# Tiles rounded to 256-byte lines, and 528 columns cut into 256 and 272

## The chip, the cores and the metric

One core of a Trainium2 chip runs the whole program. The metric is the device time of one execution in microseconds, from the chip. Three runs of the kernel before gave 2609.26, 2610.55 and 2611.42 us; the median is 2610.55 us.

## The reference

The reference is three blocks of a small language model, in float32, for one sequence of 512 tokens with a width of 1024. Sixteen learned tokens are put ahead of it for the first block, which therefore works on 528 tokens.

```
first_block:  h = h + 0.5*rmsnorm(swiglu(rmsnorm(h)))      # 528 tokens, hidden width 2816
              m = hybrid_mixer(rmsnorm(h))                 # stick-breaking and latent attention, gated
              h = h + rmsnorm(m)
              h = h + 0.5*rmsnorm(swiglu(rmsnorm(h)))      # only the 512 tokens are needed
second_block, layer 0: gated linear recurrence and matrix memory (rglru, mlstm)
              layer 1: sliding-window attention with sinks
              both:    x = x + conv_ffn(rms_norm(x))       # hidden width 3072
                       x = x + sigmoid(rms_norm(x) @ w_gate) * (p @ w_proj)
```

Nearly all of the arithmetic is products of activations with weight matrices of 1024, 2816 or 3072 rows or columns.

## The kernel before, in words

Activations lie transposed: features on the 128 partitions, in chunks of 128, and tokens along the free axis. A weight block of 128 outputs is the stationary operand, 128 by 128 for each chunk of features; the tokens are the moving operand, 512 columns at a time, or 528 columns in two equal pieces of 264 (`banks2`, L247 to L251), since a PSUM bank holds 512 columns.

Float32 accuracy comes from a split. Every operand is kept as a high and a low part of type float32r, and a product is three: high by high, high by low, low by high. So `mm` (L273) issues, per chunk of 128 features, three weight loads with three products of 512 columns; with two pieces it issues six of 264, and each of the six has its own weight load. `lin_first` (L296) is the same for the first blocks of a stage, `mm_tok` (L283) has the tokens on the stationary side. In the rows, `xh` and `xl` are the two parts of a stage's input, `whi` and `wlo` those of the weights, and a name such as `l<-xh,whi` is a product of the two into PSUM tile `l`.

Weights stream: `wdma` (L254) fetches up to 512 KB from DRAM into one of two raw buffers, ScalarE makes `whi` (L265) and VectorE makes `wlo` (L266), each with three buffers. PSUM has six banks for the large products (`l`). VectorE and ScalarE take the results out, apply the norm's factor, convolution and activation, and split the result into the two parts of the next input. GpSimd does a few multiplications and the sums of squares. All transfers are issued from the SP queue. Engines other than TensorE are ordered by a scheduler which follows program order with a priority for the weight split.

The stages, with the names of the moving operands in the rows: feed-forward 1 (`xh`, `xl`, then `hh`, `hl`; 264 columns), the mixer (`cqh`, `ysbh`, `ymh`, `ooh`), feed-forward 2 (`xh`, `hh`; 512 columns), the recurrence layer, then twice a convolution feed-forward (`xh`, then `chh`, `chl`) and a gated embedding (`xh`), and between the two of them the window attention (`yh`, `yl`).

SBUF tiles come from pools stacked from the left and from the right end of each partition, in the order in which the code opens them; each tile starts where the one before it ends, rounded up to 32 bytes. So the start of an operand depends on all small tiles ahead of it. Read from the built program, these are the starts of the float32r operands, as the rest after division by 256, and how many 512-column products have each difference (moving less stationary, rest by 256):

| operand | start before | moving less stationary | products of 512 columns |
|---|---|---|---|
| weights `whi`, `wlo` | 160 | | |
| `chh`, `chl` | 160 | 0 | 1152 |
| `ooh`, `yh`, `ymh` and their low parts, one embedding input | 224 | 64 | 504 |
| all others: `xh` and `xl` (128 or 192), `hh` of feed-forward 2 (192), `cqh`, `ysbh` and so on | several | 32, 96, 160 or 224 | 6222 |

The 3552 products of 264 columns have all eight differences, about 450 each, because a chunk of 528 columns is 2112 bytes long. The steps between chunks of 512 columns (2048 bytes) and between chunks of a weight block (512 bytes) change none of the rests.

Of the kernel before, what the change touches and what calls it, by code (L numbers as in the profile page):

```python
# [21 lines left out]
HT = TM // 2  # L22
EPS = 1e-6
# [3 lines left out]
WB = (2, 3)  # buffers of raw and of split weights  # L27
# [12 lines left out]


def _wt(w):
    """[K, N] -> [N/128, 128, K]: per block of 128 outputs, K in chunks of 128 rows on the partitions."""
    k, n = w.shape
    return np.ascontiguousarray(w.reshape(k // P, P, n // P, P).transpose(2, 1, 0, 3).reshape(n // P, P, k))


def _wr(w, per):
    """[K, N] -> [K/128/per, 128, per*N]: rows in chunks of 128 on the partitions, per chunks side by side."""
    k, n = w.shape  # L50
    return np.ascontiguousarray(w.reshape(k // P // per, per, P, n).transpose(0, 2, 1, 3).reshape(k // P // per, P, per * n))
# [6 lines left out]
def _swap(w, half):  # L58
    """Swaps the two halves of every group of 2*half columns."""
# [12 lines left out]
def prep(inp):  # L72
# [85 lines left out]
    sink = a["at_sinks_2"][0].reshape(4, 2, 2).transpose(0, 2, 1).reshape(1, 16)  # per group: heads 0, 2, 1, 3  # L158
# [5 lines left out]
def consts():  # L164
    i = np.arange(P)
    c = {}
    # stick breaking: key strictly before the query; rows are queries
    c["m_sb"] = np.where(i[None, :] < i[:, None], 0.0, NEG)
    # latent attention: a query sees its whole chunk of 64
    c["m_mla"] = np.where(i[None, :] // 64 <= i[:, None] // 64, 0.0, NEG)  # L170
    # sliding window: previous block, own block
# [21 lines left out]


class Kern:
# [4 lines left out]
    # scalar engine, with the table sets in program order  # L200
# [31 lines left out]
    # PSUM: per phase, banks for the large products (l), short-lived ones (a), scores (z)  # L232
# [14 lines left out]
    def banks2(self):  # L247
        """two banks for TM columns: matmul pieces and evacuation pieces (psum, view of a [P, TM] tile)"""
        b = [self.bank(), self.bank()]
        segs = [(b[s][:, :HT], s * HT, (s + 1) * HT) for s in range(2)]  # L250
        return segs, [(b[s][:, :HT], (lambda t, s=s: t[:, s * HT:(s + 1) * HT])) for s in range(2)]  # L251

    # weights: raw load, then an exact split in two float32r parts
# [19 lines left out]
    def mm(self, segs, w, x, kc, k0=0, m=P, first=True, last=True):  # L273
        """segs: (psum, c0, c1); w: (hi, lo) with kc chunks of m columns; x: (hi, lo) tiles [P, k, t]"""
# [8 lines left out]
    def mm_tok(self, pss, x, ws, per, n):  # L283
        """tokens on the partitions: x as the stationary side; pss: (psum, c0, c1) per block of tokens"""
# [11 lines left out]
    def lin_first(self, srcs, x, kc, c0=0, wide=False, two=False):  # L296
        """several blocks of outputs at a time, for chunks of x that are still being made: all of them (wide), or the last"""
# [19 lines left out]
    def lin2(self, src, x, kc, m=P):  # L317
        """one block of outputs over all TM tokens, in two banks: (psum, c0, c1)"""
# [6 lines left out]
    def rsqrt_small(self, pool, out, x, scale, name):  # L325
        """out = 1/sqrt(x*scale + eps) for a few columns, in the tables of exp and log, with a Newton step"""
# [12 lines left out]
    def rstd(self, acc, tt, tb, dim, pool_r, name="r"):  # L339
        """acc [P, tt]: per token sums over the partitions -> 1/sqrt(mean + eps): tokens on partitions, and broadcast in PSUM"""  # L340
# [12 lines left out]
        # pieces (psum, c0, c1)  # L353
# [10 lines left out]
    def pool(self, st, name, bufs=1, side=None, **kw):  # L364
        return st.enter_context(self.tc.tile_pool(name=name, bufs=bufs, reuse_waits="tile", side=side or self.side, **kw))

    def norm(self, hs, gname, tt, side, upd=None, tb=P):
        """Opens the next phase on a side of SBUF: x = h*g split in two parts, without the 1/rms, which fin() gives:
        n.rs broadcast [P, tt], n.rt with tokens on the partitions. upd: per chunk a call that brings h up to date"""
# [29 lines left out]
    def post(self, fs, g, hs, tt, last=None):  # L399
        """h += rmsnorm(fs)*g, as one call per chunk; the squares of the chunks are gathered here"""  # L400
# [18 lines left out]
    def begin(self, st):  # L419
        nc, d = self.nc, self.d  # L420
        self.side = "left"
        cp = self.pool(st, "cst")
# [921 lines left out]
```

## Time and profile before

| | |
|---|---|
| median of three runs | 2610.55 us |
| span of the profiled execution, first to last instruction | 2605.1 us |
| what lies around the span, against that median | 5.45 us |
| PE busy | 2554.4 us, 98% |
| weight loads (PEld) busy | 2083.0 us, 80% |
| DVE, ACT, POOL busy | 1356.4, 978.9, 311.2 us |
| mean DMA rate | 92 GB/s |

PE is the TensorE matmul queue, PEld its weight loads, DVE VectorE, ACT ScalarE, POOL GpSimd. Products are pipelined: one is listed with its whole duration although the next starts long before it ends. What a product costs in a gapless stretch is therefore the step from its start to the next start, and that is read by dividing the time between a first and a last start by the number of steps between them. A float32 product (not float32r) has two records.

### The profile page before, as it was taken

Reading aid. Unit: us, or ns where it says so; the run is one execution under the profiler, and the core shown is the slowest. Engines: PE = TensorE matmul, PEld = TensorE weight load, DVE = VectorE, ACT = ScalarE, POOL = GpSimd, SP = SyncE. Lnnn points to the kernel's source line nnn. Section 1 sums busy time; section 2 is a strip of 40 time slices with the busy share of each in tenths; the row PEclk is TensorE's granted clock in tenths of the full one; section 3 lists DMA queues with packets and bytes.
Section 4 is the critical chain, followed back from the end, with each engine's and each line's share of the span. In section 5 each row is a group of like instructions: output and inputs, shape, how many; then the busy total and the mean of one; then the engine's idle time right before and its main releaser. Section 6 shows DMA issues by size and latency. Waiting matters only on the chain.

```text
span 2605.1 us, 33169 instructions
## 1 busy us (share of the span) xinstructions
PE 2554.4 (98%) x13330; PEld 2083.0 (80%) x13334; DVE 1356.4 (52%) x2108; ACT 978.9 (38%) x1561; POOL 311.2 (12%) x250
## 2 busy tenths in 40 slices
PE   8999999999999999999999999999999899999999
PEld 8999997776667788888777788888888578888887
DVE  5333347455575642334678655355475755535544
ACT  4222234343653632223534633223343553322332
POOL 3101101011002110101100111001122111100110
PEclk9999999999999999999999999999999999999999
DMA  3222233211103323233322322332333113233232
GB/s 136 90 93 87 98 97 125 73 57 57 52 30 114 125 97 97 87 99 98 110 81 90 121 89 93 93 101 92 91 108 99 57 49 123 92 94 104 88 92 97
DMA packets 76340, 239.43 MB, mean 92 GB/s; under 512 B 9045, under 2 KB 11349, under 8 KB 75929
## 3 DMA queue, kind: packets, MB, share of 16 engines
q1 hardware_dynamic: 76184, 237.30, 28.1%
q8 instruction: 105, 1.72, 0.3%
q14 instruction: 51, 0.41, 0.1%
HBM read 225.72 MB, written 8.40 MB: 90 GB/s over the span
## 4 chain that ended last, share of the span: by engine, by line
PE 88%; DVE 5%; issue 3%; ACT 3%; POOL 1%; DMA 1%; SPq 0%; DVEq 0%; POOLq 0%; ACTq 0%
PE l L280 75%; PE l L307 3%; PE a L623 2%; PE z L647 1%; PE l L293 1%; PE a L612 1%; DVE h L226 1%; DVE xl L383 1%; PE a L361 1%; DVE wlo L266 1%; POOL gm L226 0%; ACT whi L265 0%; PE s L1250 0%; PE a L346 0%; POOL acc L226 0%
## 5 line engine op out<-in xcount | busy, mean ns | idle before, releaser
L265 ACT CAST whi<-wraw 128x1024 fp32r<-128x1024 f32 (+4 forms) x440 | 430.0, 978 | 1150.8 <-PE l L280 942.1
L280 PE MATMUL l<-xh,whi 128*128 128x512 f32 (+3 forms) x2368 | 793.7, 361 | 0.5 <-DVE sbk L226 0.5
L280 PE MATMUL l<-xl,whi 128*128 128x512 f32 (+3 forms) x2368 | 789.6, 359 | 0.0
L280 PE MATMUL l<-xh,wlo 128*128 128x512 f32 (+3 forms) x2368 | 788.4, 359 | 0.0
L266 DVE TENSOR_TENSOR wlo<-wraw,whi 128x1024 fp32r<-128x1024 f32 (+4 forms) x440 | 503.7, 1146 | 286.7 <-ACT whi L265 278.2
L280 PEld LDWEIGHTS l<-xh,whi 128*128 128x128 f32 (+1 forms) x2368 | 419.0, 188 | 75.2 <-issue 4.9
L280 PEld LDWEIGHTS l<-xh,wlo 128*128 128x128 f32 (+1 forms) x2368 | 419.6, 188 | 72.2 <-issue 1.9
L280 PEld LDWEIGHTS l<-xl,whi 128*128 128x128 f32 (+1 forms) x2368 | 419.9, 187 | 70.9 <-issue 2.0
L226 POOL TENSOR_TENSOR acc<-acc,sq 128x512 f32<-128x512 f32 (+1 forms) x63 | 98.6, 1565 | 472.4 <-ACT sq L205 435.1
L280 PE MATMUL l<-chh,whi 128*128 128x512 f32 x384 | 149.4, 389 | 0.0
L280 PE MATMUL l<-chl,whi 128*128 128x512 f32 x384 | 149.4, 389 | 0.0
L280 PE MATMUL l<-chh,wlo 128*128 128x512 f32 x384 | 149.4, 389 | 0.0
L226 POOL TENSOR_TENSOR t<-g,xrs 128x528 f32<-128x528 f32 (+1 forms) x44 | 75.6, 1718 | 571.3 <-ACT g L215 571.3
L280 PE MATMUL l<-hh,whi 128*128 128x264 f32 (+1 forms) x528 | 141.3, 322 | 0.0
L280 PE MATMUL l<-hl,whi 128*128 128x264 f32 (+1 forms) x528 | 141.1, 322 | 0.0
L280 PE MATMUL l<-hh,wlo 128*128 128x264 f32 (+1 forms) x528 | 140.7, 321 | 0.0
L226 POOL TENSOR_TENSOR cc<-cc,xrs 128x512 f32<-128x512 f32 x48 | 63.2, 1317 | 601.1 <-ACT cc L215 601.1
L226 DVE TENSOR_TENSOR t<-l,t 128x264 f32<-128x264 f32 (+1 forms) x66 | 32.3, 516 | 151.6 <-PE l L280 148.2
L226 DVE TENSOR_TENSOR cz<-l,xrs 128x512 f32<-128x512 f32 x48 | 33.2, 691 | 123.4 <-PE l L280 119.2
L226 DVE TENSOR_TENSOR g<-l,xrs 128x264 f32<-128x264 f32 (+1 forms) x66 | 32.3, 515 | 124.4 <-PE l L280 119.9
L280 PEld LDWEIGHTS l<-hl,whi 128*128 128x128 f32 x528 | 87.7, 188 | 8.1
L280 PEld LDWEIGHTS l<-hh,wlo 128*128 128x128 f32 x528 | 87.7, 188 | 8.0
(342 smaller groups left out, 3252.6 us busy)
## 6 DMA issues: line engine op xcount, KB each, us to landing
wraw<-in_up SPq DMA_DIRECT2D x96, 512.0 KB, 3.4
wraw<-in_dn SPq DMA_DIRECT2D x64, 384.0 KB, 3.1
wraw<-in_ffn_g SPq DMA_DIRECT2D x44, 512.0 KB, 3.5
wraw<-in_ffn_u SPq DMA_DIRECT2D x44, 512.0 KB, 3.4
wraw<-in_ffn_d SPq DMA_DIRECT2D x32, 448.0 KB, 3.3
wraw<-in_hy SPq DMA_DIRECT2D x20, 512.0 KB, 3.5
wraw<-in_ffn_d SPq DMA_DIRECT2D x16, 512.0 KB, 3.5
wraw<-in_gate SPq DMA_DIRECT2D x16, 512.0 KB, 3.4
```

The costliest lines, as they stand in the source:

```text
L226: return (eng or self.nc.vector).tensor_tensor(out, a, b, op=op)
L265: nc.scalar.copy(hi, raw)
L266: nc.vector.tensor_tensor(lo, raw, hi, op=ALU.subtract)
L280: self.nc.tensor.matmul(ps, a[:, k * m:(k + 1) * m], b[:, k0 + k, c0:c1], start=first and k == 0 and pi == 0, stop=last and k == kc - 1 an ...
L293: self.nc.tensor.matmul(ps[:c1 - c0, :n], a[:, k, c0:c1], b[:, j * n:(j + 1) * n], start=k == 0 and pi == 0, stop=k == nk - 1 and pi == 2)
L307: self.nc.tensor.matmul(ps, a[:, k * P:(k + 1) * P], b[:, k, t0:t1], start=k == 0 and pi == 0, stop=k == kc - 1 and pi == 2)
L361: nc.tensor.matmul(p[:, c - a:c - a + w], r[:w, i:i + 1].to_broadcast([w, P]), self.ident[:w, :w], start=True, stop=True)
L383: nc.vector.scalar_tensor_tensor(n.x[1][:, k, :], hs[k], g, n.x[0][:, k, :], op0=ALU.mult, op1=ALU.subtract)
L612: nc.tensor.transpose(pt[:kk, j * P:(j + 1) * P], probs[hh][:, i * P:i * P + kk], self.ident)
L623: nc.tensor.matmul(po[64 * hh:64 * hh + 64, :], vt[:kk, i, (2 * c + hh) * 64:(2 * c + hh + 1) * 64], where[(i, hh)], start=i == 0, stop=i ...
L647: nc.tensor.matmul(ps, q, k[:, a:b], start=True, stop=not last)
```

## The change

A class `Pool` wraps every pool that `Kern.pool` hands out. Its `tile` rounds the size of a tile up to a multiple of 256 bytes (64 float32 or 128 bfloat16 elements) and returns a view of the wanted size. Since sizes are then multiples of 256, all tiles of a side start at the same rest. On the right side a tile of 96 bytes is put at the very end, so that both sides have the rest 128. Some pools of the recurrence layer (`Y`, `R2`, `R1`, `W`) and of the window attention (`A`, `W`) keep the old sizes, by taking the inner pool. `banks2` cuts 528 columns at 256 in place of 264.

```
+CUT = T // 2
+class Pool:
+    LINE = 256
+    def __init__(self, pool):
+        self.pool = pool
+    def tile(self, shape, dtype, **kw):
+        per = self.LINE // (2 if dtype == BF16 else 4)
+        n = int(np.prod(shape[1:]))
+        if n % per == 0:
+            return self.pool.tile(shape, dtype, **kw)
+        t = self.pool.tile([shape[0], -(-n // per) * per], dtype, **kw)[:, :n]
...
     def banks2(self):
-        b = [self.bank(), self.bank()]
-        segs = [(b[s][:, :HT], s * HT, (s + 1) * HT) for s in range(2)]
-        return segs, [(b[s][:, :HT], (lambda t, s=s: t[:, s * HT:(s + 1) * HT])) for s in range(2)]
+        cuts = ((0, CUT), (CUT, TM))
+        segs = [(self.bank()[:, :b - a], a, b) for a, b in cuts]
+        return segs, [(p, (lambda t, a=a, b=b: t[:, a:b])) for p, a, b in segs]
...
     def pool(self, st, name, bufs=1, side=None, **kw):
-        return st.enter_context(self.tc.tile_pool(name=name, bufs=bufs, reuse_waits="tile", side=side or self.side, **kw))
+        return Pool(st.enter_context(self.tc.tile_pool(name=name, bufs=bufs, reuse_waits="tile", side=side or self.side, **kw)))
...
     def begin(self, st):
+        self.pool(st, "end", side="right").pool.tile([P, 24], F32, name="end")
...
-        Y = self.pool(stY, "Y", side=self.other)
+        Y = self.pool(stY, "Y", side=self.other).pool
-        R2 = self.pool(stY, "R2", side=self.other)
+        R2 = self.pool(stY, "R2", side=self.other).pool
-        R = self.pool(n.st, "R1")
+        R = self.pool(n.st, "R1").pool
...
-        A = self.pool(n.st, "A")
+        A = self.pool(n.st, "A").pool
-        W = self.pool(n.st, "W")
+        W = self.pool(n.st, "W").pool
```

The rest of the diff takes comments away. Read from the built program, after the change 7359 of the 7878 products of 512 columns have both operands at the rest 128; the other 519 have a difference of 64, 128 or 192, most of them because the mixer reads its input from the 17th column on, 64 bytes in. The products of 256 and 272 columns have differences of 0, 64, 128 and 192, about as often each. The number of instructions and their order are the same on every engine, but for one product of 512 columns in the mixer that stands eight places later in PE's order. What differs elsewhere is the size of the two pieces. On PE, in feed-forward 1 just after the broadcast of the first norm (`a<-cst,xrt`), there stood

```order
L361 MATMUL a<-cst,xrt 128x88 x6
L280 MATMUL l<-xl,whi 128x264 x2
L280 MATMUL l<-xh,wlo 128x264 x2
L280 MATMUL l<-xh,whi 128x264 x2
L280 MATMUL l<-xl,whi 128x264 x2
```

and now stands

```order
L382 MATMUL a<-cst,xrt 128x88 x6
L301 MATMUL l<-xl,whi 128x256
L301 MATMUL l<-xl,whi 128x272
L301 MATMUL l<-xh,wlo 128x256
L301 MATMUL l<-xh,wlo 128x272
L301 MATMUL l<-xh,whi 128x256
```

so each pair of equal pieces became a short and a long one, in the same place. On DVE, which takes the pieces out of PSUM (`t<-l,t` is the second factor of the gated product, `g<-l,xrs` the first), there stood, a little later in the same stage,

```order
L266 TENSOR_TENSOR wlo<-wraw,whi 128x1024
L271 TENSOR_TENSOR hl<-t,hh 128x528
L226 TENSOR_TENSOR g<-l,xrs 128x264 x2
L266 TENSOR_TENSOR wlo<-wraw,whi 128x1024
L226 TENSOR_TENSOR t<-l,t 128x264 x2
```

and now stands

```order
L287 TENSOR_TENSOR wlo<-wraw,whi 128x1024
L292 TENSOR_TENSOR hl<-t,hh 128x528
L247 TENSOR_TENSOR g<-l,xrs 128x256
L247 TENSOR_TENSOR g<-l,xrs 128x272
L287 TENSOR_TENSOR wlo<-wraw,whi 128x1024
L247 TENSOR_TENSOR t<-l,t 128x256
L247 TENSOR_TENSOR t<-l,t 128x272
```

and again only the sizes of the pieces moved; the work between them kept its place.

## Rows read from the trace of the kernel before

**Rows 1.** The page's parts 1, 2 and 4: busy time, granted clock, the last chain.
```profile
PE 2554.4 (98%) x13330; PEld 2083.0 (80%) x13334; DVE 1356.4 (52%) x2108; ACT 978.9 (38%) x1561; POOL 311.2 (12%) x250
...
PEclk9999999999999999999999999999999999999999
...
PE 88%; DVE 5%; issue 3%; ACT 3%; POOL 1%; DMA 1%; SPq 0%; DVEq 0%; POOLq 0%; ACTq 0%
PE l L280 75%; PE l L307 3%; PE a L623 2%; PE z L647 1%; PE l L293 1%; PE a L612 1%; DVE h L226 1%; DVE xl L383 1%; PE a L361 1%; DVE wlo L266 1%; POOL gm L226 0%; ACT whi L265 0%; PE s L1250 0%; PE a L346 0%; POOL acc L226 0%
```

**Rows 2.** Instructions by line and form on PE: count, then busy us, mean ns.
```profile
L280 PE MATMUL l<-xh,whi 128*128 128x512 f32 x1560 | 622.5, 399 | 0.5 <-DVE sbk L226 0.5
L280 PE MATMUL l<-xh,whi 128*128 128x264 f32 x768 | 159.9, 285 | 0.0
L280 PE MATMUL l<-chh,whi 128*128 128x512 f32 x384 | 149.4, 389 | 0.0
L280 PE MATMUL l<-hh,whi 128*128 128x264 f32 x352 | 71.8, 285 | 0.0
L280 PE MATMUL l<-hh,whi 128*128 128x512 f32 x176 | 69.5, 395 | 0.0
L280 PE MATMUL l<-ooh,whi 128*128 128x512 f32 x48 | 18.9, 394 | 0.0
```

**Rows 3.** Busy time of each engine, in stretches of the whole program.
```profile
core 0: us, PE busy (x) PEld busy (x) DVE busy (x) ACT busy (x) POOL busy (x), PEclk, DMA share, GB/s
1377.00:1450.00 73.00, 68.36 (x321) 53.32 (x320) 60.80 (x126) 38.01 (x66) 8.07 (x16) 1.00 0.28 95
1502.00:1915.00 413.00, 413.00 (x1799) 335.93 (x1798) 205.48 (x267) 125.86 (x153) 43.72 (x32) 1.00 0.30 95
1963.00:2105.00 142.00, 131.31 (x732) 90.11 (x735) 97.36 (x269) 73.98 (x230) 21.60 (x15) 1.00 0.22 67
```

**Rows 4.** What PE waited for: us in total, times, longest.
```profile
PE l L307 <- ACT xh L223: 12.8, 11, 7.6
PE l L280 <- ACT whi L265: 0.9, 1, 0.9
```

**Rows 5.** Line L280, 2290 to 2350 us: count, durations, first and last start.
```profile
L280 PE MATMUL l<-chh,wlo x89: 389/389/389, 2289.8 to 2349.6; 128*128 128x512 f32 x89
```

**Rows 6.** Line L280, 1705 to 1835 us, the same columns.
```profile
L280 PE MATMUL l<-xh,wlo x187: 395/396/396, 1704.7 to 1834.9; 128*128 128x512 f32 x187
```

**Rows 7.** Line L280, 982 to 1022 us, the same columns.
```profile
L280 PE MATMUL l<-hl,whi x58: 393/395/397, 981.7 to 1021.6; 128*128 128x512 f32 x58
```

**Rows 8.** Line L280, 845 to 875 and 808 to 826 us, the same columns.
```profile
L280 PE MATMUL l<-ooh,wlo x45: 392/392/392, 844.8 to 875.0; 128*128 128x512 f32 x45
...
L280 PE MATMUL l<-ymh,wlo x27: 394/394/394, 807.8 to 825.6; 128*128 128x512 f32 x27
```

**Rows 9.** Line L280, 160 to 235 us, the same columns.
```profile
L280 PE MATMUL l<-xh,whi x207: 282/283/291, 159.7 to 234.9; 128*128 128x264 f32 x104
L280 PE MATMUL l<-xl,whi x206: 282/286/290, 160.0 to 234.6; 128*128 128x264 f32 x103
L280 PE MATMUL l<-xh,wlo x206: 280/283/287, 160.2 to 234.8; 128*128 128x264 f32 x103
```

**Rows 10.** PE in order of time, last products: start us, us, what.
```profile
2594.61 0.28 PE L280 MATMUL l<-xh,whi 128*128 128x256 f32 x1
...
2600.10 0.28 PE L280 MATMUL l<-xh,wlo 128*128 128x256 f32 x1
```

**Rows 11.** Busy time of line L280 alone, over the whole span.
```profile
core 0: us, PE busy (x) PEld busy (x), PEclk, DMA share, GB/s
0.00:2605.10 2605.10, 2092.43 (x10512) 1735.56 (x10512) 1.00 0.28 92
```

**Rows 12.** PE in order of time, short products.
```profile
1961.80 1.00 PE L346 MATMUL a<-cst,acc 128*128 128x64 f32 x8
```

**Rows 13.** Weight transfers of the page's part 6: count, size, us to landing.
```profile
wraw<-in_up SPq DMA_DIRECT2D x96, 512.0 KB, 3.4
```

More of the change, by code (lines that the diff above doesn't have):

```diff
@@ L189, in consts @@
     return r
+class Pool:
[8 more added lines that the diff above has]
+        t = self.pool.tile([shape[0], -(-n // per) * per], dtype, **kw)[:, :n]
+        if len(shape) == 2:
+            return t
+        if len(shape) == 3:
+            return t.rearrange("p (a b) -> p a b", a=shape[1])
+        return t.rearrange("p (a b c) -> p a b c", a=shape[1], b=shape[2])
 class Kern:
@@ L920, in hy @@
         self.act(F, F, AF.Exp, scale=-1.0)
-        W = self.pool(stY, "W", side=self.other)
+        W = self.pool(stY, "W", side=self.other).pool
         gT = W.tile([P, 2, 16], F32, name="gT")
```

## The prediction

> **What bounds the kernel now.** I read the page first: PE is busy for 98% of the span at the full granted clock of 1.0 (2.4 GHz) in all 40 slices, and 88% of the chain that ended last is PE, 75% of it the one line L280 that issues the products [rows 1]. So the step from one product to the next is the time of this kernel. Then the list of PE's instructions by line and form, for the counts: L280 alone has 3 x 1560 products of `xh`, `xl` with 512 columns, 3 x 384 of `chh`, `chl`, and 3 x (768 + 352) and a few more of 264 [rows 2]. Then the busy time by stretch: from 1502 to 1915 us PE is never idle while DVE and ACT are busy for 205.48 and 125.86 of 413 us [rows 3]. PE's waits are small: the longest group is 12.8 us, at the start of stages, and weights are waited for 0.9 us in all [rows 4]. Last, what one product costs in gapless stretches, from first and last starts:
>
> - `chh`, difference 0 (moving start less stationary start, rest by 256): 2289.8 to 2349.6 us, 89 products of one of three kinds, so 88 x 3 = 264 steps: 226.5 ns. The ends are rounded to 0.1 us, which is 0.4 ns here [rows 5].
> - `xh`, difference 224: 130.2 us over 186 x 3 = 558 steps, 233.3 ns [rows 6].
> - `hl`, difference 32: 39.9 us over 57 x 3 = 171 steps, 233.3 ns [rows 7].
> - `ooh` and `ymh`, difference 64: 30.2 us over 132 steps and 17.8 us over 78, 228.8 and 228.2 ns [rows 8].
> - 264 columns, all differences mixed: 75.2 us over 618 steps, 121.7 ns [rows 9].
> - 256 columns, difference 32: 5.49 us over 47 steps, 116.8 ns [rows 10].
>
> The same instruction, with the same clock, takes 6.8 ns less where the two operands start alike, and some 5 ns less where they are alike by 64. The stage does not explain it: `xh` of 1705 to 1835 us is 233.3 next to `chh` in the same kind of feed-forward, and the `oo` and `ym` products, in other stages and from other pools, are also below 229.
>
> **The change part by part.** (1) *512 columns.* There are 7878: 1152 with difference 0, 504 with 64, 6222 with a difference that is not a multiple of 64. After it 7359 are alike, 519 differ by a multiple of 64. I take the alike step from `chh`, 226.5 ns, although both operands will start at the rest 128 and not 160: no row shows an alike pair anywhere else. The 6222 give 6222 x (233.3 - 226.5) = 42.3 us, the 504 give 504 x 2.3 = 1.2 us, and the 519 stay short of it by the same 2.3 ns, 1.2 us back. Sum 42.3 us. Bounds: nothing at all if the step stays at 233.3, a loss if it rises (the last rival); and downwards once more the same 6.8 ns if a start at 128 is better than one at 160, 7359 x 6.8 = 50 us on top.
>
> Not all of it lies on the path. The chain has 75% of the span on L280, about 1954 us [rows 1], of the 2092 us in which the line is busy [rows 11]. The rest lies in the mixer, the recurrence and the window attention, where PE also idles (68.36 of 73 us, 131.31 of 142 us busy) and DVE is occupied for two thirds of the time or more [rows 3]; there a shorter product only moves a wait. So 1954 / 2092, 93%: 42.3 x 0.93 = 39.5 us.
>
> (2) *256 and 272 in place of 264 and 264.* 3552 products make 1776 pairs, now 243.4 ns each. The columns of a pair are the same. If a column costs what 512 columns cost less 264 do, (233.3 - 121.7) / 248 = 0.45 ns, a pair of 256 and 272 is 118.1 + 125.3 = 243.4, no change; with the measured 116.8 for the short piece it is 242.1, 2.3 us in all. Among the 264s differences of every kind occur in each group of rows, and the median durations differ by 3 ns at most (283 to 286) [rows 9], so I see no gain from alikeness there. Bounds: if the short piece kept 121.7 and the long one took 125.3, 3.6 ns a pair, 6.4 us lost; if these products too gained the 6.8 ns by the column, 3.5 ns a piece, 12.4 us won. The floor of the short piece is the weight load: eight products of only 64 columns take 1.00 us with the last one's pipeline, so (1.00 - 0.27) / 7, some 104 ns each [rows 12], still under 116.8 ns. I take 1 us gained.
>
> (3) *Other products*, float32 and bfloat16 of 64 to 512 columns, 1756 records (13330 [rows 1] less 7878, 3552 and the 144 that have 256 columns before): where they are short the weight load sets their step as in [rows 12], which alignment of the moving side can't shorten. Value 0, bounds 3 ns each either way, 5 us.
>
> (4) *DVE, ACT, POOL and the transfers.* The same instructions with the same columns; evacuation of 256 and 272 is the sum of two of 264. Their starts in SBUF change. Value 0; the cover is the idle half of DVE and two thirds of ACT in the gapless stretches [rows 3]. What is late next if PE gets 3% faster: a block of 24 products then takes 24 x 0.2265 = 5.4 us, and its 512 KB land 3.4 us after issue, in two raw buffers [rows 13]; that holds.
>
> Sum: 39.5 + 1 = 40.5 us less than the profiled execution's 2605.1 us of span, 2564.6 us. The median of the runs is 5.45 us above that span (2610.55), which I keep: **2570 us**.
>
> The Trainium skill speaks against this change. Its page "SBUF — State Buffer", section "A bandwidth-pool intuition that's wrong (but worth ruling out)", gives TensorE a second, independent read port for weight loads, so where the operands lie would not matter, and by that the time would stay at 2610. The steps measured here, 226.5 and 233.3 ns, disagree [rows 5 to 7]. Its page "TensorE: Matmul & The Clock Gate", section "Back-to-back issue gap", gives N/2.4 + 2.5 ns, 215.8 ns for 512 columns; no stretch here reaches it, and if alike operands at 128 did, the 7359 would save a further 79 us by an estimate from that page alone.
>
> **The rivals.**
>
> *A start on the line is better still.* The alike pairs of today start at 160, in the middle of whatever unit the memory reads in if that is 64 bytes or more; at 128 they would start with it. For: from 264 columns to the 512 of `chh` a column costs (226.5 - 121.7) / 248 = 0.423 ns, so 226.5 holds a part of about 10 ns that is not columns, and something may come off it [rows 5, 9]. Against: no row has a start at 128 on both sides, and the 264s, of which half start on a multiple of 64, keep that part in full. Price: between half and all of the 6.8 ns for 7359 products, 25 to 50 us on top: 2520 to 2545, I say 2535.
>
> *The gain is eaten where PE is fed.* Weights, or the takers of the PSUM banks, become late in the long feed-forwards. For: six banks only, two of which go to one block in feed-forward 1. Against: the 0.9 us of waits for weights and DVE at half [rows 3, 4]. Price: half of the 40.5 us, 2590.
>
> *Placement is not the cause.* The steps follow something else that `chh`, `ooh` and `ymh` share, or the two reads never meet, and the change does nothing: 2610 us. Against it stand five stretches with one order of cost [rows 5 to 8]. This is also the outcome by the first of the two pages of the Trainium skill.
>
> *Slower: at the rest 128 alike operands meet.* Both reads then begin on the same line in the same moment, for every chunk and every weight buffer, and the one holds up the other. It decides where the alike step rises above today's mean over all 7878, (1152 x 226.5 + 504 x 228.6 + 6222 x 233.3) / 7878 = 232.0 ns. At 233.3 + 3.4, half of the known difference on the other side, it is (236.7 - 232.0) x 7359 = 35 us more, 2645. For: placement does act on the step, and this one has not been seen. Against: `chh`, alike to the byte in 88 of 88 steps of its kind, has the lowest step of all.
>
> **How the numbers follow.** Forecast 2570 with 2555 to 2582 as its own range: 0.60. Better at the line, 2535: 0.20. Half eaten, 2590: 0.07. No effect, 2610: 0.07. Slower, 2645: 0.06. A range of 2520 to 2596 leaves out the last two and a tail of the second, under 0.2. A measurement of this kernel can tell about 0.2%, 5 us, from no change. Faster by more than that: the first three, 0.87; within it: 0.07; slower: 0.06.
>
> **What would show it.** In the profile after: `xh` products of 512 columns in the convolution feed-forwards with a step of 226 to 227 ns in place of 233.3, as `chh` keeps; `ooh`, `yh` and `ymh` at the same 226 to 227; a median duration of 389 and not 395 or 396 in their rows. Pairs of 256 and 272 with 242 to 243.5 ns. PE still at 98%, waits for weights under 2 us. I am wrong if `chh` itself moves from 226.5, in either direction: then the absolute start counts and not only the difference. I am wrong too if the steps fall as forecast and the span doesn't, which would show as new waits of PE on DVE or ACT.

## The result and the profile after

Four runs of the changed kernel, beside the kernel before on the same chip: median 2578.55 us (2574.81 to 2582.27) against 2610.99 us (2609.26 to 2612.79). The ratio is 0.9874, 95% interval 0.986 to 0.9888: 32.4 us faster. Forecast were 2570 and 40.5 us less; the time lies within the forecast's own range of 2555 to 2582. The profiled execution has a span of 2577.4 us, 27.7 us less than the one before.

In the changed file the lines lie 21 or 22 further down: L280 is now L301, L307 is L328, L265 and L266 are L286 and L287. The page's parts 1, 2 and 4 of the changed kernel, as in [rows 1]:

```profile
PE 2526.4 (98%) x13330; PEld 2087.8 (81%) x13334; DVE 1355.5 (53%) x2108; ACT 978.6 (38%) x1561; POOL 312.2 (12%) x250
...
PEclk9999999999999999999999999999999999999999
...
PE 88%; DVE 5%; ACT 3%; issue 2%; POOL 1%; DMA 1%; SPq 0%; DVEq 0%; POOLq 0%; ACTq 0%
```

PE has 28.0 us less to do in as many instructions, and it is still 98% of the span; its idle time is 51.0 us for 50.7. So the difference is in the length of PE's steps, and none went into waits. The other engines' busy times moved by 1 us or less. What PE waited for, in total us, times and longest, answers to [rows 4]:

```profile
PE l L328 <- ACT xh L244: 12.5, 10, 8.0
...
PE l L301 <- ACT whi L286: 0.9, 1, 0.9
```

The same two waits, 12.5 us for 12.8 and 0.9 us as before. Next the steps. The changed kernel's products on L301, by window: count, durations (lowest, median, highest, ns), first and last start.

```profile
L301 PE MATMUL l<-chh,whi x96: 389/389/389, 1622.4 to 1687.0; 128*128 128x512 f32 x96
...
L301 PE MATMUL l<-xh,whi x192: 389/389/389, 2330.9 to 2460.8; 128*128 128x512 f32 x192
...
L301 PE MATMUL l<-hh,whi x64: 389/389/389, 979.8 to 1022.7; 128*128 128x512 f32 x64
...
L301 PE MATMUL l<-ooh,wlo x48: 389/389/389, 844.9 to 876.9; 128*128 128x512 f32 x48
...
L301 PE MATMUL l<-xl,whi x207: 275/283/288, 159.8 to 235.0; 128*128 128x272 f32 x104
L301 PE MATMUL l<-xh,wlo x206: 279/285/288, 159.9 to 234.5; 128*128 128x256 f32 x103
```

Worked out as in the prediction, one less than the count, times three kinds: `chh` 64.6 us over 285 steps, 226.7 ns (226.5 in [rows 5]); `xh` 129.9 over 573, 226.7 (233.3 in [rows 6]); `hh` 42.9 over 189, 227.0 (233.3 for its low part in [rows 7]); `ooh` 32.0 over 141, 227.0 (228.8 in [rows 8]). The rounded ends make 0.2 to 0.7 ns of that; by unrounded starts all four are 226.7. Every median is 389. And the pieces of 528 columns: 75.2 us over 618 steps, 121.7 ns, the same as in [rows 9].

So the steps did what was forecast, and yet the span fell by 12.8 us less than the sum of 40.5 (the median by 8 us less). Two things stand in that. First the clock. The busy time of the changed kernel by stretch (columns as in [rows 3]):

```profile
core 0: us, PE busy (x) PEld busy (x) DVE busy (x) ACT busy (x) POOL busy (x), PEclk, DMA share, GB/s
20.00:40.00 20.00, 17.04 (x133) 16.82 (x132) 9.28 (x12) 7.81 (x11) 8.24 (x5) 0.91 0.28 82
...
829.00:845.00 16.00, 13.18 (x49) 10.15 (x50) 7.06 (x11) 5.54 (x8) 6.10 (x3) 0.89 0.50 170
1440.00:1455.00 15.00, 12.25 (x59) 9.65 (x58) 8.44 (x35) 8.56 (x27) 0.00 (x0) 0.89 0.10 34
...
1963.00:2105.00 142.00, 133.27 (x681) 87.87 (x683) 93.44 (x262) 74.24 (x227) 18.83 (x13) 0.96 0.21 60
```

The granted clock is 1.00 there in the profile before (for the last line see [rows 3]). The trace gives it as 0.5, the lower of the two levels (1.2 and not 2.4 GHz), from 26.8, 835.8, 1443.4 and 2003.1 us for 3.4 us each, and from 2044.1 for 6.8 us. The forty slices of the page are too coarse to show it. PE in order of time around the second of these:

```profile
833.25 0.39 PE L328 MATMUL l<-ooh,wlo 128*128 128x512 f32 x1
835.74 0.78 PE L328 MATMUL l<-ooh,whi 128*128 128x512 f32 x1 [2.09 <-ACT ooh L291]
836.46 0.79 PE L328 MATMUL l<-ool,whi 128*128 128x512 f32 x1
837.05 0.63 PE L328 MATMUL l<-ooh,wlo 128*128 128x512 f32 x1
837.48 0.63 PE L328 MATMUL l<-ooh,whi 128*128 128x512 f32 x1
...
839.18 0.40 PE L328 MATMUL l<-ool,whi 128*128 128x512 f32 x1
839.42 0.40 PE L328 MATMUL l<-ooh,wlo 128*128 128x512 f32 x1
```

PE idles for 2.09 us, until ScalarE has made `ooh`; then the steps are 0.43 us and not 0.23, and at 839.2 they are back. The steps that touch these stretches cost 6.4 us more than the same steps before: 4.3 us in gapless steps of the first three, and 2.1 us in two steps of the window attention, which hold the stretches from 2003.1 and 2044.1 us together with idle time and short products. Those two take 7.39 and 51.36 us against 6.82 and 49.87 before, and 6.81 and 49.85 in a second profile of the changed kernel that has the full clock there (experiment 7). Whether the change makes the stretches is asked below.

The rest is what the steps really gained. Each of the 11573 steps between the starts of two float32r products can be set against the same step before. The order is the same but for one piece of the mixer, of 264 columns before and 272 after, which stands eight products earlier (it is this one that moved, and not a product of 512 columns). A step is called gapless here when no other instruction of PE stands in it and it is under 260 ns in both profiles:

| steps | count | change of one, ns | sum, us |
|---|---|---|---|
| 512 columns, difference 32, 160 or 224 before, 0 after, gapless | 5486 | -6.2 | -34.0 |
| 512 columns, 64 before, 0 after, gapless | 481 | -2.0 | -0.9 |
| 512 columns, not a multiple of 64 before, 64 to 192 after, gapless | 409 | -0.5 | -0.2 |
| 512 columns, 0 before and after, gapless | 1152 | -0.1 | -0.1 |
| 512 columns, not gapless | 331 | | +0.2 |
| 256, 264 and 272 columns | 3678 | | +0.4 |
| all that touch a stretch at half the clock | 36 | | +6.4 |

The sum is -28.1 us, and without the last row the steps gained 34.5 us. Against the forecast's terms, 12.4 us are missing: 4.4 us on the gapless 512-column steps (35.1 for 39.5), 1.4 on the pieces, 0.2 on steps that are not gapless, and 6.4 by the clock.

### The profile page after: what moved, and what is told of

Its sections match the earlier page's. It is cut to its first block, busy times and chain, and to the rows that moved or that the text cites. A ratio compares the mean times of both kernels' runs of the same rounds, so it can differ in the third digit from the quotient of the medians.

```text
span 2577.4 us, 33167 instructions
## 1 busy us (share of the span) xinstructions
PE 2526.4 (98%) x13330; PEld 2087.8 (81%) x13334; DVE 1355.5 (53%) x2108; ACT 978.6 (38%) x1561; POOL 312.2 (12%) x250
## 4 chain that ended last, share of the span: by engine, by line
PE 88%; DVE 5%; ACT 3%; issue 2%; POOL 1%; DMA 1%; SPq 0%; DVEq 0%; POOLq 0%; ACTq 0%
PE l L301 75%; PE l L328 3%; PE a L645 2%; PE z L669 1%; PE l L314 1%; PE a L634 1%; DVE h L247 1%; DVE xl L404 1%; PE s L1272 1%; PE a L382 1%; PE a L1294 0%; POOL gm L247 0%; DVE wlo L287 0%; PE a L1300 0%; ACT whi L286 0%
## 5 line engine op out<-in xcount | busy, mean ns | idle before, releaser
L286 ACT CAST whi<-wraw 128x1024 fp32r<-128x1024 f32 (+4 forms) x440 | 430.3, 979 | 1115.2 <-PE l L301 911.0
L301 PE MATMUL l<-xh,whi 128*128 128x512 f32 (+3 forms) x2368 | 785.5, 357 | 0.5 <-DVE sbk L247 0.5
L301 PE MATMUL l<-xh,wlo 128*128 128x512 f32 (+3 forms) x2368 | 780.9, 356 | 0.0
L301 PE MATMUL l<-xl,whi 128*128 128x512 f32 (+3 forms) x2368 | 780.7, 355 | 0.0
L287 DVE TENSOR_TENSOR wlo<-wraw,whi 128x1024 fp32r<-128x1024 f32 (+4 forms) x440 | 503.4, 1145 | 283.8 <-ACT whi L286 272.7
L301 PEld LDWEIGHTS l<-xh,whi 128*128 128x128 f32 (+1 forms) x2368 | 421.3, 188 | 66.1 <-issue 4.8
L301 PEld LDWEIGHTS l<-xh,wlo 128*128 128x128 f32 (+1 forms) x2368 | 420.7, 188 | 63.7 <-issue 1.9
L301 PEld LDWEIGHTS l<-xl,whi 128*128 128x128 f32 (+1 forms) x2368 | 421.5, 188 | 62.3 <-issue 2.1
L301 PE MATMUL l<-chh,whi 128*128 128x512 f32 x384 | 149.4, 389 | 0.0
L301 PE MATMUL l<-chl,whi 128*128 128x512 f32 x384 | 149.4, 389 | 0.0
L301 PE MATMUL l<-chh,wlo 128*128 128x512 f32 x384 | 149.4, 389 | 0.0
L301 PE MATMUL l<-hh,wlo 128*128 128x256 f32 (+2 forms) x528 | 140.1, 320 | 0.0
L301 PE MATMUL l<-hh,whi 128*128 128x256 f32 (+2 forms) x528 | 140.0, 319 | 0.0
L301 PE MATMUL l<-hl,whi 128*128 128x256 f32 (+2 forms) x528 | 139.8, 319 | 0.0
L247 DVE TENSOR_TENSOR t<-l,t 128x256 f32<-128x256 f32 (+1 forms) x66 | 32.3, 516 | 148.1 <-PE l L301 144.8
L247 DVE TENSOR_TENSOR g<-l,xrs 128x256 f32<-128x256 f32 (+1 forms) x66 | 32.3, 516 | 122.2 <-PE l L301 116.2
L301 PEld LDWEIGHTS l<-hh,whi 128*128 128x128 f32 x528 | 88.3, 188 | 6.9
L301 PEld LDWEIGHTS l<-hh,wlo 128*128 128x128 f32 x528 | 88.1, 188 | 6.9
L301 PEld LDWEIGHTS l<-hl,whi 128*128 128x128 f32 x528 | 88.1, 188 | 6.8
```

The costliest lines, as they stand in the source:

```text
L247: return (eng or self.nc.vector).tensor_tensor(out, a, b, op=op)
L286: nc.scalar.copy(hi, raw)
L287: nc.vector.tensor_tensor(lo, raw, hi, op=ALU.subtract)
L301: self.nc.tensor.matmul(ps, a[:, k * m:(k + 1) * m], b[:, k0 + k, c0:c1], start=first and k == 0 and pi == 0, stop=last and k == kc - 1 an ...
```

## The experiments

**The theory.** A step's length hangs on where the moving operand starts less where the weights start, rest by 256 bytes, and at 0 it is the least. **Rivals:** the start on a line counts, for one operand or both; the cut into 256 and 272 counts; something else in the layout counts (banks that engines share, other tiles); the small gain at 64 is a step of a ladder that goes on beyond 0.

**1. The weights later by 32 bytes.** All is rounded as in the change, but the weights' pool starts 32 bytes later, so no product is alike: of those that were, nearly all have the difference 224, and the few in which the weights are the moving operand have 32.

```
     def begin(self, st):
...
+        self.pool(st, "pad").pool.tile([P, 8], F32, name="pad")
         self.wp = self.pool(st, "wp")
+        self.pool(st, "pad2").pool.tile([P, 56], F32, name="padb")
```

> The changed kernel with the weight tiles 32 bytes later, so that 7260 of the 7878 products of 512 columns have a difference of 224 (none is alike), all else as changed. Theory (the difference of the starts sets the step): 226.7 to 233.3 ns for some 7300 products, times the 0.93 of the line that lies on the path, 45 us more than the changed kernel: about 2623 us, somewhat over the kernel before. Rival (rounding to 256-byte lines helps as such, wherever the weights lie): it stays at 2579 us.

Measured: 2621.24 us (2619.29 to 2627.0, six runs), ratio 1.0037, 1.0025 to 1.0048: the whole gain is gone. It is 8.5 us above the kernel before, beside which it ran: `chh` now loses 1152 x 6.6 = 7.6 us, and the 481 steps that had 64 lose 4.4 ns each, 2.1 us. Its `chh` products, columns as above:

```profile
L301 PE MATMUL l<-chl,whi x88: 395/396/396, 2299.7 to 2360.6; 128*128 128x512 f32 x88
L301 PE MATMUL l<-chh,wlo x88: 395/396/396, 2300.0 to 2360.9; 128*128 128x512 f32 x88
```

60.9 us over 261 steps, 233.3 ns and not 226.7, and a median of 396. Rounding without likeness brings nothing, so the sizes and other tiles are out.

**2. Both later by 32 bytes.** The tile at the right end is 64 bytes long, and one of 32 bytes is put ahead of everything on the left: all starts have the rest 160 and the differences stay.

```
-        self.pool(st, "end", side="right").pool.tile([P, 24], F32, name="end")
+        self.pool(st, "end", side="right").pool.tile([P, 16], F32, name="end")
+        self.pool(st, "pad").pool.tile([P, 8], F32, name="pad")
```

> The changed kernel with all rounded tiles 32 bytes later on both sides, so that the operands start at the rest 160 and their differences are as changed. Theory (only the difference counts): 2578 us within 3 us, with steps of 226.7 ns. Rival (a start at 128 is part of the gain): 2590 us or more.

Measured: 2579.55 us (2576.86 to 2582.83, four runs), ratio 0.9872, 0.9852 to 0.9891, the changed kernel's. Its `xh`:

```profile
L301 PE MATMUL l<-xh,whi x141: 389/389/389, 2344.7 to 2439.9; 128*128 128x512 f32 x141
```

95.2 us over 420 steps, 226.7 ns. A common start at 160 does as well as one at 128; only the difference shows.

**3. Rounding alone, and the cut alone.** In the one the changed kernel cuts 528 at 264 again; in the other the kernel before cuts at 256.

```
-CUT = T // 2
+CUT = HT
```

> The changed kernel with 528 columns cut at 264 again: the rounding alone. Theory: a pair costs 243.4 ns however it is cut, so 2579 us within 3 us, with steps of 226.7 ns for 512 columns. Rival (the uneven cut is behind the lower mean granted clock of the changed kernel, 0.996 against 1.000): clock 1.000 and 2571 us. Rival (the uneven cut is part of the gain): 2583 us or more.

```
-        b = [self.bank(), self.bank()]
...
+        cuts = ((0, T // 2), (T // 2, TM))
+        segs = [(self.bank()[:, :b - a], a, b) for a, b in cuts]
```

> The kernel before with 528 columns cut at 256 and nothing rounded. Theory: no difference, 2611 us within 3 us, steps of 233.3 ns for 512 columns. Rival (the uneven cut lowers the granted clock here and there): clock 0.996 and 2618 us.

Measured: rounding alone 2578.51 us (2576.05 to 2580.35, four runs), ratio 0.987, 0.9856 to 0.9885; the cut alone 2615.12 us (2611.48 to 2617.53, ten runs), ratio 1.001, 1.0 to 1.002. The cut gives nothing that the times could tell, on either layout; the gain is the rounding's. The cut alone is 2.4 us above the kernel before beside it, 1 us beyond the range that was expected. The rival that the uneven cut lowers the granted clock has no support: its mean is 0.9964 in these ten runs and 0.9969 in the fifteen of the kernel before beside them, and 0.9975 in the four of rounding alone, where the rival wanted 1.000. Rounding alone, in the stretch of [rows 9]:

```profile
L301 PE MATMUL l<-xh,wlo x206: 281/285/289, 159.8 to 234.8; 128*128 128x264 f32 x103
```

103 pairs, from the first piece of the first to the second of the last 102 x 6 + 1 = 613 steps in 75.0 us, 122.4 ns. That is 0.7 ns more than in the kernel before and in the changed one, 121.7 both, and 0.7 x 3552 = 2.5 us in all: the rounding made the pieces of 264 a little dearer, and the cut took that back. In the kernel with the cut alone the same stage has 122.0 ns, 1.1 us in all. These are differences below what the times show, and only the steps show them.

**4. The steps by themselves.** A small kernel, which computes nothing of the reference, loads two float32r tiles and issues groups of 48 products, each group with other starts; the weights are eight blocks in turn.

```
nc.tensor.matmul(p, b[:, wo + j * P:wo + (j + 1) * P], a[:, mo:mo + n], ...)
```

> No part of the reference is computed: groups of 48 products of 128x128 float32r weights with 512 moving columns, one after another, each group with its own distance between the two operands; weights go through eight chunks 512 bytes apart. Theory (only the difference by 256 counts): 226.7 ns a product at 0, about 229 at 64 bytes, 232 to 233.5 at the other multiples of 32, and the same 226.7 in all eight groups in which both operands move together by 32 bytes. Rival (the absolute start counts): the groups that move together differ by 3 ns or more. For 256, 264 and 272 columns: alike and 32 bytes off within 1 ns of each other, near 117, 121 and 125 ns. For bfloat16 and float32 operands the theory has no number; if the port for 4-byte columns at one a cycle is the cause, bfloat16 (2 bytes) and float32 (slower columns) show no dependence on the difference.

Its rows: `da`, `dc`, `de` have the moving operand later by 0, 32 and 64 bytes, `wb` and `wg` the weights later by 32 and by 192; `nac` and `nuc` have 256 columns at 0 and 32; `hc` and `hd` are bfloat16 at 64 and 96 bytes, `fb` and `fc` float32 at 32 and 64.

```profile
L39 PE MATMUL da<-x,w x48: 389/389/389, 18.0 to 28.7; 128*128 128x512 f32 x48
...
L39 PE MATMUL dc<-x,w x48: 393/396/399, 40.0 to 51.0; 128*128 128x512 f32 x48
...
L39 PE MATMUL de<-x,w x48: 387/392/397, 62.4 to 73.2; 128*128 128x512 f32 x48
...
L39 PE MATMUL wb<-x,w x48: 392/395/397, 294.4 to 305.4; 128*128 128x512 f32 x48
...
L39 PE MATMUL wg<-x,w x48: 388/392/397, 350.4 to 361.2; 128*128 128x512 f32 x48
...
L39 PE MATMUL nac<-x,w x48: 281/283/304, 394.0 to 399.6; 128*128 128x256 f32 x48
L39 PE MATMUL nuc<-x,w x48: 278/280/284, 399.8 to 405.3; 128*128 128x256 f32 x48
...
L39 PE MATMUL hc<-xb,wb x48: 379/379/379, 500.3 to 510.4; 128*128 128x512 bf16 x48
L39 PE MATMUL hd<-xb,wb x48: 379/379/379, 510.6 to 520.8; 128*128 128x512 bf16 x48
...
L39 PE MATMUL fb<-xf,wf x48: 592/592/592, 541.6 to 561.8; 128*128 128x512 f32 x48
L39 PE MATMUL fc<-xf,wf x48: 592/592/592, 562.2 to 582.4; 128*128 128x512 f32 x48
```

The medians of the kernel come back: 389 alike, 396 at 32, 392 at 64. By unrounded starts, ns a step:

| difference, bytes | 0 | 32 | 64 | 96 | 128 | 160 | 192 | 224 | 240 |
|---|---|---|---|---|---|---|---|---|---|
| 512 columns, moving later | 226.7 | 233.4 | 229.1 | 233.6 | 232.5 | 234.2 | 233.2 | 233.4 | 226.8 |

Weights later by 192 bytes is the same rest as moving later by 64, and it gives 229.0 ns; weights later by 96, 128 and 160 give 234.2, 232.5 and 233.4, as moving later by 160, 128 and 96 do within 0.2 ns. So it is the rest by 256 that counts. Both operands later together by 0 to 224 bytes: 227.2 to 227.5, which the first steps of a group make; between its ninth and 41st start each of the eight groups has 226.7. bfloat16: 215.8 to 216.0 at all four differences. Float32: 429.2 for each of a product's two records, at all four. With fewer columns the order changes, against the expectation that 256, 264 and 272 columns would not tell the difference by more than 1 ns: 256 columns take 120.3 alike and 117.9 at 32, 264 take 120.3 and 121.9, 272 take 125.5 at both, 320 and 384 differ by 0.1, and 448 take 206.4 alike and 204.4 at 32. So the step is set by both starts together, but "alike" is no rule of its own: it is best at 512 columns. That two reads meet is a reading of this; no run shows the reads themselves.

**5. Finer steps.** The same kernel with starts 4 bytes apart, and other shapes.

> No part of the reference is computed: more groups of 48 float32r products. The moving operand later by 4 bytes a step, the stationary one later by 4 bytes a step; stationary columns 2, 3 or 4 elements apart; moving columns in two runs with a gap; one weight chunk again and again; 264, 256 and 480 columns at eight differences. Theory (weight reads and moving reads meet at the same memory place, counted by 256 bytes): a step changes smoothly or in small jumps with the difference, 226.7 ns at 0 and no distance below about 226; stationary columns 2 or more apart sweep the places faster and lose the good case: 230 ns or more in both of their groups. Rival (some distance avoids the meetings altogether): a group near the 215.8 ns of bfloat16, which would be worth 10 ns on 7359 products, 80 us.

Moving later by 4, 20 and 28 bytes (`db`, `df`, `dh`), and 264 columns at 192 and 224 (`pg`, `ph`):

```profile
L42 PE MATMUL db<-x,w x48: 395/398/401, 31.6 to 42.8; 128*128 128x512 f32 x48
...
L42 PE MATMUL df<-x,w x48: 399/404/405, 76.3 to 87.6; 128*128 128x512 f32 x48
...
L42 PE MATMUL dh<-x,w x48: 387/387/393, 99.0 to 109.7; 128*128 128x512 f32 x48
...
L42 PE MATMUL pg<-x,w x48: 278/284/296, 545.9 to 551.6; 128*128 128x264 f32 x48
L42 PE MATMUL ph<-x,w x48: 281/282/289, 551.7 to 557.3; 128*128 128x264 f32 x48
```

From 0 to 44 bytes: 226.7, 236.6, 233.1, 228.9, 231.7, 239.9, 233.5, 226.8, 233.3, 234.7, 233.2, 230.0 ns. It is no ladder of 16 or 64 bytes; single distances such as 28 and 240 are as good as 0, and none is better. The rival that a distance exists which spares more than likeness does fell here, as far as 512 columns were tried: nothing lies below 226.7. Weights 2 to 4 elements apart are not faster either (233.2 to 235.4 alike, 233.5 to 236.6 at 32).

**6. A version after the numbers.** For 264 columns the small kernel gave 120.3, 121.9, 120.9, 121.7, 123.5, 121.8, 120.55 and 120.15 ns at differences of 0 to 224 in steps of 32. The second piece of 264 columns starts 1056 bytes after the first, so its difference is 32 higher. The pair of 192 and 224 takes 240.7 ns; only 224 and 0 is as low, 240.45, and it was not run. So the chunks of 528 columns are put 2304 bytes apart, each with 48 unused columns ahead of it, and 528 is cut at 264.

```
+    def spaced(self, pool, k, tt, name):
+        lead = 48 if tt == TM else 0
+        return pool.tile([P, k, lead + tt], F32R, name=name)[:, :, lead:]
...
-        n.x = [xp.tile([P, KD, tt], F32R, name=nm) for nm in ("xh", "xl")]
+        n.x = [self.spaced(xp, KD, tt, nm) for nm in ("xh", "xl")]
```

and the same for `hh` and `hl`.

> The changed kernel, with the chunks of the 528-column operands (xh, xl of feed-forward 1 and of the mixer, hh, hl of feed-forward 1) 2304 bytes apart in place of 2112, their first column 64 bytes below the weights' place in a line (a difference of 192), and 528 columns again in two pieces of 264. So 1752 pairs of products have the differences 192 and 224 (before they had all), and 384 more products of 512 columns, which the mixer takes from the 17th column on, are alike. Theory (a step's length is set by the columns and by moving less stationary, rest by 256, alone): the steps measured by themselves give 120.55 + 120.15 = 240.7 ns a pair against 121.7 + 121.7 = 243.4 in the changed kernel: 1752 x 2.7 = 4.7 us less, and up to 384 x 2.4 = 0.9 us for the mixer's products, of which most stand in stretches that wait; about 2573.5 us if the changed kernel stands at 2578.5. Rival (the steps in a real stage are set by something that the small kernel doesn't have, the traffic of the other engines, so that differences other than 0 don't repeat there): pairs at 242 to 244 ns as now, 2577 to 2580 us.

Measured: 2570.06 us (2568.23 to 2577.08, five runs), ratio to the kernel before 0.9846, 0.9833 to 0.9858. The changed kernel on the same chip had 2576.61 us, 0.9853 to 0.9884 of the kernel before, so this one is 6.5 us below it by the medians, 5.6 were expected; the two intervals overlap by a little. Set against runs of the changed kernel of the same granted clock (the table of experiment 7), its runs at 0.996 to 0.999 are 5.9 to 7.3 us lower, each of the four. Feed-forward 1 in the stretch of [rows 9]:

```profile
L301 PE MATMUL l<-xh,whi x210: 279/283/284, 160.1 to 235.1; 128*128 128x264 f32 x105
L301 PE MATMUL l<-xh,wlo x210: 279/283/284, 159.8 to 234.8; 128*128 128x264 f32 x105
```

105 pairs; from the first piece of the first to the second of the last 104 x 6 + 1 = 625 steps in 75.0 us, 120.0 ns for 121.7. So the steps of the small kernel hold in a real stage, where DVE and ACT work beside PE, and the rival that they don't repeat fell for this pair of differences. This is the best version that was run.

**7. Both kernels again, for the clock.** First the kernel before without an edit, then the changed one.

> The kernel before, unchanged, once more with a profile. Theory (the falls of the granted clock at the starts of stages come and go from one execution to the next, whatever the kernel): a mean clock of 0.996 to 0.998 and falls of 3.4 us in the first stage, at the gated sum of the mixer or in the window attention, at a span of 2608 to 2612 us. Rival (the kernel before has none): clock 1.000 and a span of 2605 us again.

> The changed kernel once more, without an edit, beside the one with spaced chunks on the same chip. Theory: 2576 to 2581 us; steps as in its first profile (226.7 ns for the alike products, 243.4 for a pair of 256 and 272 columns). Of the stretches at half the clock (granted clock 0.5) that its first profile shows at 26.8, 835.8, 1443.4, 2003.1 and 2044.1 us: if they belong to the layout, they stand at the same places again; if they come and go from one execution to the next, some are gone and the span differs by 1 to 2 us for each.

Measured: before again 2612.68 us (2606.31 to 2615.84, eight runs), ratio 1.0008, 0.9997 to 1.0019; its profile, with a span of 2604.5 us, has one stretch at half the clock, from 1406.2 us, in the recurrence layer. That is neither the 0.996 to 0.998 nor one of the places that were expected of it (its mean is 0.999), and not the rival's clock without a fall either. Changed again 2576.61 us (2573.67 to 2587.47, five runs); its profile has two, from 25.3 and 878.7, not five, and a span of 2573.5 us for 2577.4. At the place shown above the same kernel now has nearly the same idle time, 2.07 us, and keeps the clock:

```profile
834.62 0.50 PE L328 MATMUL l<-ooh,whi 128*128 128x512 f32 x1 [2.07 <-ACT ooh L291]
835.34 0.51 PE L328 MATMUL l<-ool,whi 128*128 128x512 f32 x1 [0.22 <-DVE ool L292]
835.68 0.40 PE L328 MATMUL l<-ooh,wlo 128*128 128x512 f32 x1
835.92 0.40 PE L328 MATMUL l<-ooh,whi 128*128 128x512 f32 x1
```

Here the steps are 0.22 to 0.24 us from the third product on. In the window attention, too, the clock is full (columns as in [rows 3], the granted clock third from the end):

```profile
1963.00:2105.00 142.00, 131.93 (x693) 87.78 (x692) 96.72 (x265) 75.21 (x229) 19.42 (x14) 1.00 0.21 63
```

So the stretches come and go from one execution to the next at a few places where PE has just idled. Whether the change makes them more frequent can be read from the mean granted clock of every timed run:

| granted clock | before: runs, mean us | changed: runs, mean us | difference |
|---|---|---|---|
| 0.995 | 5, 2615.3 | 1, 2582.3 | -33.0 |
| 0.996 | 11, 2613.3 | 1, 2579.2 | -34.1 |
| 0.997 | 16, 2612.1 | 3, 2577.4 | -34.7 |
| 0.998 | 6, 2611.4 | 1, 2575.3 | -36.1 |
| 0.999 | 8, 2608.3 | 1, 2574.8 | -33.5 |

The 47 runs of the kernel before go from 0.994 to 0.999, the changed kernel's nine from 0.992 to 1.0, and the mean of either is 0.997: no more of it after than before, as far as nine runs can tell. At an equal clock the change is worth 33 to 36 us, each difference from one to three runs of the changed kernel, and the steps outside the stretches gave 34.5. What the clock takes is in both kernels. The profile before, at 1.000, is an execution in which none of it was to be seen, so the two spans compare an execution at the full clock with one at 0.996.

## Why the prediction was right, point by point

*What bounds the kernel, and the mechanism:* right. The steps follow the difference of the two starts; moving only the weights takes it all away (experiment 1), moving both changes nothing (2), and the small kernel, where next to nothing else runs, gives the same 226.7, 233.4 and 229.1 ns (4).

*Term (1), 39.5 us from 512 columns:* the mechanism right, the size too large by 4.4 us. Measured are 34.0 + 0.9 + 0.2 = 35.1 us. The term had 6222 x 6.8 ns, times 0.93. 6222 x 0.93 = 5786 steps were to gain 6.8 ns; 5486 gained 6.2. One part is that of the 519 that do not become alike. The forecast gave them the 228.6 ns of the difference 64, as if every multiple of 64 were half alike; 128 and 192 cost 232.5 and 233.2 (experiment 4), and the 409 among them that had been unlike gained 0.5 ns. They lie in the mixer, and no row before showed a 128 or a 192: the step was extended from one difference to its multiples. Even the 96 that went from 32 to 64 stand at 232.7 ns (233.0 before), and not at the 228.9 that `ooh` and its like had at 64 before; why is open. The other part is the gain of one step, 6.2 and not 6.8: 0.2 ns because the alike step is 226.7, the rest because between blocks and at the borders of stages a step is longer after too (227.0 to 227.2 in the mean of all gapless steps). That the products in stretches that wait would give nothing was right: those that are not gapless changed by 0.2 us outside the half clock.

*Term (2), 1 us from the cut:* nothing, and inside the bounds. The pair is 243.4 ns before and after, made of two things that the term did not have: the rounding made the pieces of 264 dearer by 0.7 ns, and the cut took that back (experiment 3). The 116.8 ns for 256 columns stood at the difference 32, where the small kernel has 117.9; alike it has 120.3, and 125.5 for 272, so it could not be carried over; in feed-forward 1 of the changed kernel the two pieces take 118.4 and 124.9. The floor of 104 ns was misread too: the eight records of [rows 12] are four float32 products of two records each. Float32r products of 128 and 192 columns take 110.5 to 112.3 ns in the small kernel, which is still under the short piece. Experiment 6 shows that the pieces do have something to give, 3.4 ns a pair, by their differences and not by the cut, which the prediction denied ("I see no gain from alikeness there"). It read that from medians over mixed differences, and these were too coarse for 1 to 3 ns.

*Terms (3) and (4), nothing from other products and engines:* right. Busy times of DVE, ACT and POOL stayed within 1 us, the wait for weights at 0.9 us, and bfloat16 and float32 products of 512 columns show no dependence at the four differences that were tried.

*The base of 5.45 us around the span:* right in its use and wrong in its name. In every run with both figures 1.7 to 1.9 us lie around the span. The other 3.6 us fit the clock: the profiled execution had 1.000 throughout, and runs of the kernel before at 0.998 take 2611.4 us; the clock of the three runs ahead of the prediction is not on record. Kept as an allowance it gave the right base, since the changed kernel's runs lose as much; that was luck, for nothing in the prediction was about the clock. Of the 8.1 us by which the medians fell short of 40.5, the terms (1) and (2) and the steps that are not gapless make 6.0; the other 2 are within what the clock changes from run to run.

*The rivals.* "A start on the line is better still" fell by experiment 2, "placement is not the cause" by 1 and 4, "alike operands meet at 128" by the result itself, `chh` being 226.7 at 128 and at 160. "The gain is eaten where PE is fed" (2590) would also leave the gain short of 40.5, but PE's waits did not grow. The Trainium skill's page "SBUF — State Buffer", section "A bandwidth-pool intuition that's wrong (but worth ruling out)", by which the weight loads have a read port of their own, agrees with bfloat16 here, 215.8 to 216.0 ns at the four differences tried, and disagrees with float32r (226.7 to 239.9). For bfloat16 the Trainium skill's page "TensorE: Matmul & The Clock Gate", section "Back-to-back issue gap", gives 512 / 2.4 + 2.5 = 215.8 ns, which the small kernel shows; its float32r products of 512 columns never come below 226.7.

What stays open: a stage with all eight differences mixed has 121.7 or 122.4 ns for 264 columns, while the mean of the eight steps measured one by one is 121.4; what the order of differences adds was not measured. Also what the two operands share on their way into PE. The steps show that the two starts act together, and differently from one 4-byte start to the next, and not where. Why one idle time of 2.1 us is followed by half the clock in one execution and not in the next is open too.

## What to carry to other kernels

Where PE runs float32r products back to back, divide first and last starts of gapless stretches into steps and sort them by the difference of the two operands' starts: here 2.9% of a step, and 1.3 to 1.5% of the time, hung on nothing but where tiles and chunks start. Measure the difference that a layout will have for the very column count it will have, since what is best at 512 columns is not at 256 or 264. And set two profiles against each other at an equal granted clock: runs of the changed kernel lay 13.8 us apart, at 0.992 and at 1.0.

## What the runs showed of the hardware

The step depends on the distance of moving and stationary operand to 4 bytes: 226.7 ns at 0, 236.6 at 4, 239.9 at 20, 226.8 at 28 (512 columns, float32r). With 256 columns the unlike starts are the faster ones, 117.9 against 120.3, with 448 too, 204.4 against 206.4. bfloat16 products (215.8 to 216.0) and float32 products (429.2 a record) of 512 columns don't show it at 0, 32, 64 and 96 bytes. Float32r moving columns two elements apart take 452.9 ns and four apart 461.3, twice the 226.7 of adjoining ones.
